# An encoder layer on one core: own PSUM banks for the attention outputs, a second buffer for post-norm scales, longer down steps, and x read directly by ScalarE

## The chip, the cores and the metric

The kernel runs on one core of a Trainium2 chip. The metric is the device time of one execution in microseconds (us), lowest being best. A core has a matrix engine (TensorE, PE in the profile), a vector engine (VectorE, DVE), an engine for functions and copies (ScalarE, ACT), GpSimd (POOL), and SyncE (SP), whose queue issues nearly all transfers from HBM here. Matmul results land in PSUM, which this kernel divides into eight banks of 128 x 512 f32; all else lives in SBUF.

## What is computed

One layer of an encoder for 256 tokens of width 2048. A SwiGLU feed-forward (inner width 5632), a token mixer with 16 heads of 128 (4 of neighbourhood attention, 12 of a mixture of dilated windows), a second feed-forward, and a gated per-layer input, each between two RMS norms with gains:

```python
for i in range(DEPTH):                                  # DEPTH = 1
    f = _swiglu(_rmsnorm(h, ffn1_pre_g[i]), ffn1_w_gate[i], ffn1_w_up[i], ffn1_w_down[i])
    h = h + 0.5 * _rmsnorm(f, ffn1_post_g[i])
    m = _mixer(_rmsnorm(h, mix_pre_g[i]), w_qkv[i], na_rpb[i], out_g[i], w_o[i])
    h = h + _rmsnorm(m, mix_post_g[i])
    f = _swiglu(_rmsnorm(h, ffn2_pre_g[i]), ffn2_w_gate[i], ffn2_w_up[i], ffn2_w_down[i])
    h = h + 0.5 * _rmsnorm(f, ffn2_post_g[i])
    g = jax.nn.sigmoid(_rmsnorm(h, ple_pre_g[i]) @ w_ple_gate[i])
    h = h + _rmsnorm(g * (p[i] @ w_ple_proj[i]), ple_post_g[i])
```

In the mixer, q, k and v come from one projection; the heads' outputs o are normalised per head, scaled by `out_g` and multiplied by `w_o`.

## The kernel before

The tokens stand in two tiles of 128 (t = 0 and 1); the layer's weights, 373 MB with everything, are streamed from HBM once. A **k-tile** is 128 rows of a weight matrix; a product has 512 columns of output at a time, one PSUM bank for each token tile.

*Products.* To keep f32 accuracy, each operand is split into a rounded high part and the low rest. `load_rows` fetches four k-tiles (1 MB) into `raw`; `split` makes `wh` (a cast on ScalarE, L72) and `wl` (a subtraction on VectorE, L73), two k-tiles at a time, six buffers of each. `mac` then does three matmuls per k-tile and token tile (L90 high x high, L91 low x high, L92 high x low). `product` walks over the k-tiles in steps: by default eight k-tiles, a shorter one first if they don't divide. In each step it does t = 0, then t = 1. A caller may give other `steps`, and a job `mid`: that is put into the last step, three k-tiles before t = 1 is done, when t = 0 is complete.

*Pair product.* From the second block on, gate and up of 512 columns each are computed together by `pair_product`, which needs fewer products of half size by adding weights and inputs first, in the manner of Strassen. It has accumulators x, v, z and y, and four times a temporary product named `pair_x` that ScalarE copies out (L174 and a later line) or VectorE adds in. All of them take a bank from the pool `ps_acc`.

*Feed-forward.* `swiglu` goes through 11 blocks of 512 hidden columns in groups of 3, 3, 3 and 2. Behind each group come the down products of its hidden columns, for four blocks b of output columns, with steps of four k-tiles (`KB`) each. `down_out` adds a result to f (L396); in the last group it also sums squares (L232) and multiplies f by the post-norm scale `g_post` (L399), which `gain` loads for each block (L217) into the pool `gpool` with one buffer.

*Seams.* When the last block of t = 0 is complete, `residual` begins: a sum (L225), a power on GpSimd (L226 and L227), h = f*r + h (L328), then `transposed_split`: transposes of h on PE (L239), the product y_g with the next pre-norm gain (L243), and the split into u_h (L245) and u_l (L246), which the next products read. After the first feed-forward the next product is q; after the second it is pp, the product with the per-layer input, which does not read h, and then the gate pg, which does.

*Mixer.* For each of four groups g of four heads, products q, k and v are computed and rotated or scaled, then `attend` runs: for each token tile and pair of heads, scores `sc` (L504), bias and maximum on VectorE (L511), exponentials `pr` on ScalarE (L515), transposes `pt` (L521), a copy `pts` on ScalarE (L523) and the product `o` with v (L527). Scores and transposes share the two banks of `ps_tr`; o takes a bank of `ps_acc`. The result `on` is transposed and split later. Behind the last group stand the products `mo` with `w_o`.

*Start.* The first gate product loads x as it goes (`load_x`, in steps of 1, 1 and seven times 2 k-tiles): xb arrives by DMA, VectorE multiplies it by the gain (xg, L297), ScalarE casts (u_h, L298), VectorE subtracts (u_l, L299). The first two xg are kept for `token_sums`, the input sums of the pair products.

*Order.* The program is written in this sequence, but each engine's order is set by the framework's scheduler from the order of writing, the pools' free buffers and its own priorities. So a pool with another number of buffers can move instructions on an engine.

Of the kernel before, what the change touches and what calls it, by code (L numbers as in the profile page):

```python
# [8 lines left out]
F32 = mybir.dt.float32  # L9
# [6 lines left out]
P = 128  # L16
D = 2048
S = 256
# [15 lines left out]
def encoder_layer(ctx: ExitStack, tc: tile.TileContext, a: dict, out: bass.AP):  # L34
# [9 lines left out]
    resid = ctx.enter_context(tc.tile_pool(name="resid", bufs=1))  # L44
    acts = ctx.enter_context(tc.tile_pool(name="acts", bufs=1))
    wpool = ctx.enter_context(tc.tile_pool(name="wpool", bufs=3))
    gpool = ctx.enter_context(tc.tile_pool(name="gpool", bufs=1))
    work = ctx.enter_context(tc.tile_pool(name="work", bufs=2))
    small = ctx.enter_context(tc.tile_pool(name="small", bufs=4))
    ps_acc = ctx.enter_context(tc.tile_pool(name="ps_acc", bufs=6, space=PSUM))  # L50
    ps_tr = ctx.enter_context(tc.tile_pool(name="ps_tr", bufs=2, space=PSUM))


    ident = const.tile([P, P], F32, name="ident")
# [81 lines left out]
    def pair_product(lhs, sums, wa, ca, wb, cb):  # L136

        a11, a12 = of_tile(lhs[:2], 0), of_tile(lhs[2:4], 0)
        a22 = of_tile(lhs[2:4], 1)  # L150
        s1, s2, s3, s4 = sums
        nk = len(lhs)

        def bank(x):
            return ps_acc.tile([P, NB], F32, name=f"pair_{x}", tag="acc")

        def part(name):
            return ffn_pool[0].tile([P, NB], F32, name=name, tag="part", bufs=6)

        def add(out_, x, y):  # L160
            nc.vector.tensor_tensor(out_, x, y, op=ALU.add)  # L161

        def rest(w, k, c, accs_, first=False, last=False):

            parts = load_parts(w, k * P, 4, c)
            for t, acc in accs_:
                mac(acc, of_tile(lhs[k : k + 4], t), parts, first=first, last=last)

        ra = load_rows(wa, 0, 4, ca, pool=ffn_pool[0], bufs=2)
        rb = load_rows(wb, 0, 4, cb, pool=ffn_pool[0], bufs=2)  # L170
        x = bank("x")
        mac(x, a11, split(ra[:, :2]), first=True, last=True)
        p1 = part("p1")
        nc.scalar.copy(p1, x)  # L174
        add(ra[:, :2], ra[:, :2], rb[:, :2])
        x = bank("x")
        mac(x, s1, split(ra[:, :2]), first=True, last=True)
        r5 = part("r5")
        nc.scalar.copy(r5, x)
        v, z = bank("v"), bank("z")  # L180
        rest(wb, 4, cb, [(1, v), (0, z)], first=True)
        run_later()
        add(ra[:, :2], ra[:, :2], rb[:, 2:])
        x = bank("x")
        mac(x, s2, split(ra[:, :2]), first=True, last=True)
        w_ = part("w")
        add(w_, x, p1)
        mac(z, s4, split(rb[:, 2:]))
        add(rb[:, 2:], rb[:, :2], rb[:, 2:])
        rest(wb, 8, cb, [(1, v), (0, z)])  # L190
        x = bank("x")
# [97 lines left out]
    def load_x(k):  # L289
        if k % 2:  # L290
            return
        hi, lo = (u[:, k % KB : k % KB + 2] for u in x_blocks[k // KB])
        xb = work.tile([P, 2, S], F32, name="xb", tag="hg")
        nc.sync.dma_start(xb, xT[:, k : k + 2])
        xg = work.tile([P, 2, S], F32, name="xg", tag="y0" if k < KB else "sq")
        g = row_g[:, 0, k : k + 2]
        nc.vector.tensor_tensor(xg, xb, g.unsqueeze(2).broadcast_to([P, 2, S]), op=ALU.mult)  # L297
        nc.scalar.copy(hi, xg)  # L298
        nc.vector.tensor_tensor(lo, xg, hi.bitcast(F32), op=ALU.subtract)  # L299
        if k < KB:  # L300
            x_first.append(xg)

    def load_h(k):
        t = k // KB - NT
# [40 lines left out]
    def swiglu(pool, f, ssf, res, blocks, rs, sums, w_gate, w_up, w_down, g_post):  # L345
# [11 lines left out]
        for gi, ng in enumerate(FF_GROUPS):  # L357
            hid = []
            for nb in range(f0, f0 + ng):
# [4 lines left out]
                else:  # L364
                    gate, up = accs("gate"), accs("up")
                    if rs is None:
                        steps = [1, 1] + [2] * 7
                        product(gate, lhs, w_gate, 0, c0, steps=steps, ahead=load_x)
                        a1, a2 = x_first
                        half = [slice(t * P, (t + 1) * P) for t in range(NT)]  # L370
                        sums += token_sums(*(x[:, :, h_] for h_ in half for x in (a1, a2)))
# [15 lines left out]
            for b in range(D // NB):  # L387
# [15 lines left out]
                    if last and b == D // NB - 1:  # L403
                        next(res)

                product(acc, hrows, w_down, f0 * NB, b * NB, steps=[KB] * ng, mid=mid)
                down_out(1)
            f0 += ng

# [15 lines left out]
    with ExitStack() as att:  # L425
# [66 lines left out]
        def attend(qT, kT, v, bias, o_split, g):  # L492

            for t in range(NT):
                tok = slice(t * P, (t + 1) * P)
                o = ps_acc.tile([P, KB, HD], F32, name="o", tag="acc")
                den = small.tile([P, KB], F32, name="den")
                for h0 in range(0, KB, 2):
                    sc = ps_tr.tile([P, 2, S], F32, name="sc", tag="tr")
# [43 lines left out]
                    on, o, ro.unsqueeze(2).broadcast_to([P, KB, HD]), op=ALU.mult  # L543
                )
                on = on.rearrange("p h d -> p (h d)")
                later.append(lambda on=on, t=t: transposed_split(on, *o_split, t, g))

        w_na, w_dil = 4 * HD, 12 * HD
        o_blocks = []
# [182 lines left out]
```

## Time and profile before

| | us |
|---|---|
| three runs | 1986.32, 1985.33, 1981.21 (median 1985.33) |
| the profiled execution | 1985.5 |
| its span from the first to the last instruction | 1983.5 |
| PE busy | 1947.0 (98%) |
| VectorE busy | 1371.2 (69%) |
| ScalarE busy | 992.0 (50%) |
| weights and inputs read from HBM | 373.33 MB, 189 GB/s over the span |

The mean granted clock of TensorE is 0.995. The span divides into the first feed-forward (to about 726 us), the mixer (to about 1146), the second feed-forward (to about 1867) and the per-layer input.

A line of the timeline gives its start and duration in us, the engine, the line of the kernel, the operation, its output and inputs with their shapes, and, in brackets, how long the engine stood idle before it and what released it. A matmul's duration there holds its latency, so that records of neighbours overlap; the pace is the distance of their starts. Names such as `pair_x` or `g_post` are those of tiles in the kernel.

### The profile page before, as it was taken

To read this page: it belongs to the slowest core of one execution; us is meant where nothing else is said; L and a number is where in the kernel's file an instruction comes from. 1 tells how busy PE (TensorE), PEld (TensorE's weight loads), DVE (VectorE), ACT (ScalarE), POOL (GpSimd) and SP (SyncE) were. 2 spreads that over 40 slices of the span, in tenths; PEclk is the share of its full clock that TensorE was granted. 3 is DMA by queue.
4 is the path that set the end of the run, shared out by engine and by line. 5 is a ranking of instruction groups with operands and counts; after the bars stand their busy time and mean duration, and the time that the engine had idled before them with its cause. 6 is when DMAs were issued, how large, how long until landed. Compare 5 with 4: busy or idle time off the path is not lost.

```text
span 1983.5 us, 22804 instructions
## 1 busy us (share of the span) xinstructions
PE 1947.0 (98%) x8840; PEld 1612.7 (81%) x8840; DVE 1371.2 (69%) x1526; ACT 992.0 (50%) x1206; POOL 26.5 (1%) x47
## 2 busy tenths in 40 slices
PE   8999999999999999999999999999999999999998
PEld 6888888888888878788888878888888888888786
DVE  6874787578757776566565587747875787577764
ACT  6554554355435446544535465545543554354563
POOL 0000000000000000000000000000000000000000
PEclk9999999999999999999999999999999999999999
DMA  9666556555655546454453665555565556555453
GB/s 336 212 211 201 170 191 226 177 191 170 233 170 191 191 163 214 130 198 139 138 202 127 219 211 186 210 198 171 191 229 174 191 170 233 170 190 191 170 195 119
DMA packets 190348, 376.91 MB, mean 190 GB/s; under 512 B 6432, under 2 KB 9504, under 8 KB 189984
## 3 DMA queue, kind: packets, MB, share of 16 engines
q1 hardware_dynamic: 190240, 375.46, 55.8%
q8 instruction: 69, 1.13, 0.2%
q14 instruction: 39, 0.32, 0.0%
HBM read 373.33 MB, written 2.10 MB: 189 GB/s over the span
## 4 chain that ended last, share of the span: by engine, by line
PE 95%; DMA 2%; ACT 1%; DVE 1%; issue 0%; POOL 0%; SPq 0%; DVEq 0%; POOLq 0%; ACTq 0%
PE down L90 8%; PE down L91 8%; PE down L92 8%; PE pair_x L90 5%; PE pair_x L91 5%; PE pair_x L92 5%; PE pair_z L92 3%; PE pair_y L90 3%; PE pair_z L90 3%; PE pair_z L91 3%; PE pair_y L92 3%; PE pair_y L91 3%; PE pair_v L90 3%; PE pair_v L91 3%; PE pair_v L92 3%; PE tr L239 2%
## 5 line engine op out<-in xcount | busy, mean ns | idle before, releaser
L73 DVE TENSOR_TENSOR wl<-raw,wh 128x1024 fp32r<-128x1024 f32 (+1 forms) x753 | 908.9, 1221 | 446.0 <-ACT wh L72 421.8
L72 ACT CAST wh<-raw 128x1024 fp32r<-128x1024 f32 (+1 forms) x753 | 790.0, 1052 | 762.2 <-PE down L91 207.9
L90 PE MATMUL down<-wh,hid_h 128*128 128x512 f32 x704 | 274.7, 391 | 0.1
L91 PE MATMUL down<-wh,hid_l 128*128 128x512 f32 x704 | 274.2, 389 | 0.0
L92 PE MATMUL down<-wl,hid_h 128*128 128x512 f32 x704 | 274.2, 389 | 0.0
L90 PEld LDWEIGHTS down<-wh,hid_h 128*128 128x128 f32 x704 | 132.2, 188 | 28.1 <-ACT hid_h L245 1.0
L92 PEld LDWEIGHTS down<-wl,hid_h 128*128 128x128 f32 x704 | 132.2, 188 | 27.4
L91 PEld LDWEIGHTS down<-wh,hid_l 128*128 128x128 f32 x704 | 132.2, 188 | 27.1
L90 PE MATMUL pair_x<-wh,u_h 128*128 128x512 f32 x320 | 124.6, 389 | 0.0
L91 PE MATMUL pair_x<-wh,u_l 128*128 128x512 f32 x320 | 124.6, 389 | 0.0
L92 PE MATMUL pair_x<-wl,u_h 128*128 128x512 f32 x320 | 124.6, 389 | 0.0
L90 PE MATMUL pair_y<-wh,u_h 128*128 128x512 f32 x280 | 109.0, 389 | 0.0
L92 PE MATMUL pair_y<-wl,u_h 128*128 128x512 f32 x280 | 109.0, 389 | 0.0
L91 PE MATMUL pair_y<-wh,u_l 128*128 128x512 f32 x280 | 109.0, 389 | 0.0
L161 DVE TENSOR_TENSOR raw<-raw 128x1024 f32<-128x1024 f32 x80 | 97.8, 1223 | 1.4
L92 PE MATMUL pair_z<-wl,u_h 128*128 128x512 f32 x240 | 93.5, 390 | 0.0
L90 PE MATMUL pair_z<-wh,u_h 128*128 128x512 f32 x240 | 93.4, 389 | 0.0
L91 PE MATMUL pair_z<-wh,u_l 128*128 128x512 f32 x240 | 93.4, 389 | 0.0
L91 PE MATMUL pair_v<-wh,u_l 128*128 128x512 f32 x240 | 93.4, 389 | 0.0
L92 PE MATMUL pair_v<-wl,u_h 128*128 128x512 f32 x240 | 93.4, 389 | 0.0
L90 PE MATMUL pair_v<-wh,u_h 128*128 128x512 f32 x240 | 93.4, 389 | 0.0
L92 PEld LDWEIGHTS pair_x<-wl,u_h 128*128 128x128 f32 x320 | 60.1, 188 | 12.5
(195 smaller groups left out, 3085.3 us busy)
## 6 DMA issues: line engine op xcount, KB each, us to landing
raw<-in_ffn_w_up SPq DMA_DIRECT2D x88, 1024.0 KB, 5.1
raw<-in_ffn_w_down SPq DMA_DIRECT2D x88, 1024.0 KB, 4.9
raw<-in_ffn_w_gate SPq DMA_DIRECT2D x84, 1024.0 KB, 5.1
raw<-in_w_qkv SPq DMA_DIRECT2D x48, 1024.0 KB, 5.1
raw<-in_w_o SPq DMA_DIRECT2D x16, 1024.0 KB, 4.9
raw<-in_w_ple_gate SPq DMA_DIRECT2D x16, 1024.0 KB, 5.0
raw<-in_ffn_w_gate SPq DMA_DIRECT2D x7, 512.0 KB, 4.8
xb<-in_xT SPq DMA_DIRECT2D x8, 256.0 KB, 4.2
```

Of the source, the lines that this page charges most:

```text
L72: nc.scalar.copy(wh[:, :n], raw)
L73: nc.vector.tensor_tensor(wl[:, :n], raw, wh[:, :n].bitcast(F32), op=ALU.subtract)
L90: nc.tensor.matmul(acc, xh, wh, start=lead, stop=False)
L91: nc.tensor.matmul(acc, xl, wh, start=False, stop=False)
L92: nc.tensor.matmul(acc, xh, wl, start=False, stop=tail)
L161: nc.vector.tensor_tensor(out_, x, y, op=ALU.add)
L239: nc.tensor.transpose(tr[:, k], x[:, k * P : (k + 1) * P], ident)
```

## The change

Five things change.

1. `gpool` has two buffers instead of one.
2. `ps_acc` has four banks instead of six, and a new pool `ps_o` has the two others. The attention outputs o take theirs from `ps_o`, and so do the four temporaries of `pair_product` (`pair_x` before, `pair_s` now).
3. `load_x`: the product xg is gone. ScalarE's activation scales xb by the gain and rounds it to u_h, per k-tile, and VectorE gets u_l as xb*g - u_h in one operation per k-tile. The first two xb are multiplied by the gain in place, ahead of `token_sums`.
4. The down products keep steps of four k-tiles only for the first block of columns; the others have the default: 4 and 8 k-tiles in groups of three, 8 in the last group.
5. `on`, transposed, uses another buffer tag (`y0`).

```diff
-    gpool = ctx.enter_context(tc.tile_pool(name="gpool", bufs=1))
+    gpool = ctx.enter_context(tc.tile_pool(name="gpool", bufs=2))
...
-    ps_acc = ctx.enter_context(tc.tile_pool(name="ps_acc", bufs=6, space=PSUM))
+    ps_acc = ctx.enter_context(tc.tile_pool(name="ps_acc", bufs=4, space=PSUM))
     ps_tr = ctx.enter_context(tc.tile_pool(name="ps_tr", bufs=2, space=PSUM))
+    ps_o = ctx.enter_context(tc.tile_pool(name="ps_o", bufs=2, space=PSUM))
...
         def bank(x):
+            if x == "s":
+                return ps_o.tile([P, NB], F32, name="pair_s", tag="o")
             return ps_acc.tile([P, NB], F32, name=f"pair_{x}", tag="acc")
...
-        x = bank("x")
+        x = bank("s")
         mac(x, a11, split(ra[:, :2]), first=True, last=True)
...
-        xb = work.tile([P, 2, S], F32, name="xb", tag="hg")
+        xb = work.tile([P, 2, S], F32, name="xb", tag="y0" if k < KB else "hg")
         nc.sync.dma_start(xb, xT[:, k : k + 2])
-        xg = work.tile([P, 2, S], F32, name="xg", tag="y0" if k < KB else "sq")
-        g = row_g[:, 0, k : k + 2]
-        nc.vector.tensor_tensor(xg, xb, g.unsqueeze(2).broadcast_to([P, 2, S]), op=ALU.mult)
-        nc.scalar.copy(hi, xg)
-        nc.vector.tensor_tensor(lo, xg, hi.bitcast(F32), op=ALU.subtract)
+        for i in range(2):
+            g = row_g[:, 0, k + i : k + i + 1]
+            nc.scalar.activation(hi[:, i], xb[:, i], AF.Copy, scale=g)
+            nc.vector.scalar_tensor_tensor(
+                lo[:, i], xb[:, i], g, hi[:, i].bitcast(F32), op0=ALU.mult, op1=ALU.subtract
+            )
         if k < KB:
-            x_first.append(xg)
+            x_first.append(xb)
...
+                        for i, x in enumerate(x_first):
+                            g = row_g[:, 0, 2 * i : 2 * i + 2].unsqueeze(2).broadcast_to([P, 2, S])
+                            nc.vector.tensor_tensor(x, x, g, op=ALU.mult)
...
-                product(acc, hrows, w_down, f0 * NB, b * NB, steps=[KB] * ng, mid=mid)
+                product(acc, hrows, w_down, f0 * NB, b * NB, steps=[KB] * ng if b == 0 else None, mid=mid)
...
-                o = ps_acc.tile([P, KB, HD], F32, name="o", tag="acc")
+                o = ps_o.tile([P, KB, HD], F32, name="o", tag="o")
...
-                later.append(lambda on=on, t=t: transposed_split(on, *o_split, t, g))
+                later.append(lambda on=on, t=t: transposed_split(on, *o_split, t, g, tag="y0"))
```

The change moves instructions at these places (line numbers after it are larger by 1 to 7: L90 to L92 are L91 to L93, L239 is L242, L504 is L511, L521 is L528, L527 is L534).

PE in the second attention (g = 1), before: the rows from the last scores of the first pair of heads to the second token tile; q stands only further down, behind the third o.

```order
L504 MATMUL sc<-kT_l,qT_h 128x256
L521 MATMUL pt<-ident,pr 128x128 x2
L504 MATMUL sc<-kT_h,qT_h 128x256
L504 MATMUL sc<-kT_h,qT_l 128x256
L504 MATMUL sc<-kT_l,qT_h 128x256
L521 MATMUL pt<-ident,pr 128x128 x2
L504 MATMUL sc<-kT_h,qT_h 128x256
L504 MATMUL sc<-kT_h,qT_l 128x256
L504 MATMUL sc<-kT_l,qT_h 128x256
L527 MATMUL o<-v,pts 128x128 x4
```

The same place now, from the fourth of six q matmuls that stand ahead of the first pt (q is the next group's product, which only reads u and weights):

```order
L91 MATMUL q_6787<-wh,u_h 128x512
L92 MATMUL q_6787<-wh,u_l 128x512
L93 MATMUL q_6787<-wl,u_h 128x512
L528 MATMUL pt<-ident,pr 128x128 x2
L511 MATMUL sc<-kT_h,qT_h 128x256
L511 MATMUL sc<-kT_h,qT_l 128x256
L528 MATMUL pt<-ident,pr 128x128 x2
L511 MATMUL sc<-kT_l,qT_h 128x256
L511 MATMUL sc<-kT_h,qT_h 128x256
L511 MATMUL sc<-kT_h,qT_l 128x256
L511 MATMUL sc<-kT_l,qT_h 128x256
L91 MATMUL q_6787<-wh,u_h 128x512
```

Six q matmuls moved ahead of pt, and further ones stand one by one before and between the groups of o. In the first attention (g = 0) twelve stand ahead of pt.

PE at the end of the second feed-forward, before: the last down matmuls, the products pp with the per-layer input, and the first transposes of the new h.

```order
L91 MATMUL down_13924<-wh,hid_l 128x512
L92 MATMUL down_13924<-wl,hid_h 128x512
L90 MATMUL pp_14038<-wh,p_h 128x512
L91 MATMUL pp_14038<-wh,p_l 128x512
L92 MATMUL pp_14038<-wl,p_h 128x512
L90 MATMUL pp_14038<-wh,p_h 128x512
L91 MATMUL pp_14038<-wh,p_l 128x512
L92 MATMUL pp_14038<-wl,p_h 128x512
L90 MATMUL pp_14039<-wh,p_h 128x512
L91 MATMUL pp_14039<-wh,p_l 128x512
L239 MATMUL tr<-ident,h 128x128 x4
```

The same place now:

```order
L91 MATMUL down_13929<-wh,hid_h 128x512
L92 MATMUL down_13929<-wh,hid_l 128x512
L242 MATMUL tr<-ident,h 128x128 x4
L93 MATMUL down_13929<-wl,hid_h 128x512
L242 MATMUL tr<-ident,h 128x128 x4
L91 MATMUL down_13929<-wh,hid_h 128x512
L92 MATMUL down_13929<-wh,hid_l 128x512
L93 MATMUL down_13929<-wl,hid_h 128x512
L91 MATMUL pp_14043<-wh,p_h 128x512
```

The transposes of the first tile's h moved from behind eight pp matmuls to four matmuls ahead of the end of the down products. The end of the first feed-forward has them at the like place.

VectorE at the start, before:

```order
L297 TENSOR_TENSOR xg<-xb,row_g 128x512 x2
L299 TENSOR_TENSOR u_l<-xg,u_h 128x512
L73 TENSOR_TENSOR wl<-raw,wh 128x512 x2
L299 TENSOR_TENSOR u_l<-xg,u_h 128x512
L73 TENSOR_TENSOR wl<-raw,wh 128x1024
L297 TENSOR_TENSOR xg<-xb,row_g 128x512
L299 TENSOR_TENSOR u_l<-xg,u_h 128x512
L297 TENSOR_TENSOR xg<-xb,row_g 128x512
L73 TENSOR_TENSOR wl<-raw,wh 128x1024
```

And now (y_s and sums_l belong to `token_sums`):

```order
L301 SCALAR_TENSOR_TENSOR u_l<-xb,row_g,u_h 128x256 x2
L375 TENSOR_TENSOR xb<-xb,row_g 128x512
L74 TENSOR_TENSOR wl<-raw,wh 128x512 x2
L301 SCALAR_TENSOR_TENSOR u_l<-xb,row_g,u_h 128x256 x2
L74 TENSOR_TENSOR wl<-raw,wh 128x1024
L301 SCALAR_TENSOR_TENSOR u_l<-xb,row_g,u_h 128x256 x4
L375 TENSOR_TENSOR xb<-xb,row_g 128x512
L258 TENSOR_TENSOR y_s<-xb 128x256
L260 TENSOR_TENSOR y_s<-xb 128x256
L259 TENSOR_TENSOR y_s<-y_s,xb 128x256
L261 TENSOR_TENSOR y_s<-xb,y_s 128x256
L264 TENSOR_TENSOR sums_l<-y_s,sums_h 128x512
```

The token sums moved ahead of the second subtraction of 128x1024 weights; before they stood far behind. On SP the third and fourth load of x are issued earlier, and each `g_post` one place earlier.

More of the change, by code (lines that the diff above doesn't have):

```diff
@@ L175, in pair_product @@
         add(ra[:, :2], ra[:, :2], rb[:, :2])
-        x = bank("x")
+        x = bank("s")
         mac(x, s1, split(ra[:, :2]), first=True, last=True)
@@ L183, in pair_product @@
         add(ra[:, :2], ra[:, :2], rb[:, 2:])
-        x = bank("x")
+        x = bank("s")
         mac(x, s2, split(ra[:, :2]), first=True, last=True)
@@ L190, in pair_product @@
         rest(wb, 8, cb, [(1, v), (0, z)])
-        x = bank("x")
+        x = bank("s")
         mac(x, s3, split(rb[:, 2:]), first=True, last=True)
```

## The prediction

> **What bounds the kernel now.** I read the page's busy times first, then the view of stretches (the windows), then PE's waits grouped by releaser, then the timeline around each wait.
>
> ```profile
> span 1983.5 us, 22804 instructions
> PE 1947.0 (98%) x8840; PEld 1612.7 (81%) x8840; DVE 1371.2 (69%) x1526; ACT 992.0 (50%) x1206; POOL 26.5 (1%) x47
> 0.00:35.00 35.00, 27.15 (x104) 20.98 (x104) 24.20 (x33) 19.12 (x24) 0.73 (x7) 1.00 0.90 307
> 690.00:760.00 70.00, 66.36 (x294) 53.72 (x293) 53.74 (x71) 37.99 (x63) 5.19 (x8) 0.95 0.57 193
> 800.00:825.00 25.00, 21.70 (x121) 18.62 (x120) 11.29 (x30) 13.87 (x28) 2.03 (x2) 0.93 0.27 85
> 1175.00:1850.00 675.00, 674.95 (x3023) 559.69 (x3022) 488.05 (x491) 336.79 (x363) 0.00 (x0) 1.00 0.57 193
> 1850.00:1900.00 50.00, 46.62 (x216) 38.36 (x215) 37.06 (x49) 28.43 (x50) 4.03 (x6) 0.97 0.51 171
> ```
>
> A row of stretches gives its bounds and length, then the busy time of PE, PEld, DVE, ACT and POOL, PE's granted clock, the DMA share and GB/s. TensorE is busy for 98% of the span. Inside the second feed-forward (1175 to 1850) it is busy for 674.95 of 675 us at clock 1.00, so nothing can be had there without fewer matmuls, and the change removes none. What can be won is idle time and half clock at the seams: the start, the end of each feed-forward (690:760 and 1850:1900), and the attentions (800:825 is the first). The clock dips in just these stretches. The prices:
>
> ```profile
> 719.75 0.39 PE L90 MATMUL down<-wh,hid_h 128*128 128x512 f32 x1
> 726.32 0.39 PE L92 MATMUL down<-wl,hid_h 128*128 128x512 f32 x1
> 729.80:733.30 3.50, 2.25 (x6) 1.32 (x7) 3.50 (x7) 1.84 (x4) 0.00 (x0) 0.50 0.01 2
> 733.80 0.63 PE L90 MATMUL q<-wh,u_h 128*128 128x512 f32 x1
> 734.23 0.63 PE L91 MATMUL q<-wh,u_l 128*128 128x512 f32 x1
> ```
>
> The first two are the first and last of 30 matmuls in a row: 6.57 us over 29 steps, **0.2266 us per matmul**. At clock 0.50 the step is 0.43, so each matmul loses 0.20.
>
> **The change part by part.** Let T be the end of the last down matmul, 726.55 in the first feed-forward.
>
> *End of the first feed-forward.* PE's next work there is q, whose input needs the finished h.
>
> ```profile
> 724.03 0.69 DVE L396 TENSOR_TENSOR f<-f,down 128x512 f32<-128x512 f32 x1 [0.63 <-PE down L92]
> 726.17 0.15 DVE L225 TENSOR_REDUCE m<-ssf 128x1 f32<-128x4 f32 x1
> 728.17 1.41 DVE L328 SCALAR_TENSOR_TENSOR h<-f,r,h 128x512 f32<-128x512 f32 x2 [0.44 <-POOL r L227]
> 729.02 1.71 PE L239 MATMUL tr<-ident,h 128*128 128x128 f32 x8 [2.31 <-issue]
> 730.10 1.37 DVE L243 TENSOR_TENSOR y_g<-tr,row_g 128x512 f32<-128x512 f32 x2
> 731.56 0.80 PE L90 MATMUL q<-wh,u_h 128*128 128x512 f32 x1 [0.82 <-ACT u_h L245]
> 732.78 0.80 PE L91 MATMUL q<-wh,u_l 128*128 128x512 f32 x1 [0.42 <-DVE u_l L246]
> 737.43 0.60 PE L239 MATMUL tr<-ident,h 128*128 128x128 f32 x4
> ```
>
> The first token tile's sums end before the last 12 matmuls now (4 k-tiles of 3), and before the last 24 with a last step of 8 k-tiles. The whole chain of that tile therefore starts 12 x 0.2266 = 2.72 us earlier: reduce at T-3.1, h at T-1.1, first transpose at T-0.25 instead of T+2.5. The order puts three h updates ahead of y_g instead of two, so y_g stands at T-1.1+3x0.69 = T+1.0 (was T+3.55), q's first matmul 1.46 behind that at T+2.4 (was T+5.0). Before u_l DVE now does two y_g, the second tile's f and one h (2.1 and 0.7): u_l at T+3.7, the second q matmul at T+4.4 (was T+6.2). Up to the second tile's transposes 15 q matmuls stand (13 now): PE is there at T+4.4+14x0.23 = T+7.6 if warm, 1.4 later if seven of these are at half clock; now it is at 737.43 = T+10.9. That is 3.3 or 1.9 less, and two matmuls more (0.45): 3.7 or 2.3. A transpose that waits for one of the two banks that scores and transposes share may cost 0.7. Its price isn't in the trace, so bounds: **2.6 us, between 1.6 and 3.7**. The idle time left is about 2 us ahead of q and 1.6 behind its first matmul, near to the 2.31 and 0.82 that brought clock 0.50, so I lean to the half clock. The Trainium skill, "TensorE: Matmul & The Clock Gate", section "Part 1: The HAM clock gate", says that the gate falls to half only after an idle window of about 3.4 us; by that no half clock would come here, and this term would be its upper end. The trace differs: PE was idle 2.5 us and then 1.2 when it fell at 729.8.
>
> *The four attentions.* Now o takes two of six accumulator banks, and q of the next group has none free until o is read. With banks of its own for o, q's matmuls can fill the holes.
>
> ```profile
> 805.09 0.28 PE L504 MATMUL sc<-kT_l,qT_h 128*128 128x256 f32 x1
> 808.07 0.47 PE L521 MATMUL pt<-ident,pr 128*128 128x128 f32 x2 [2.70 <-ACT pr L515]
> 808.10:811.80 3.70, 3.67 (x17) 3.37 (x18) 0.78 (x4) 1.93 (x7) 0.00 (x0) 0.54 0.99 323
> 887.26 0.28 PE L504 MATMUL sc<-kT_l,qT_h 128*128 128x256 f32 x1
> 888.82 0.44 PE L521 MATMUL pt<-ident,pr 128*128 128x128 f32 x2 [1.28 <-ACT pr L515]
> 890.51 1.16 PE L527 MATMUL o<-v,pts 128*128 128x128 f32 x8 [0.32 <-ACT pts L523]
> 895.84 1.16 PE L527 MATMUL o<-v,pts 128*128 128x128 f32 x8 [0.38 <-ACT pts L523]
> 887.00:897.00 10.00, 7.83 (x60) 6.94 (x59) 5.74 (x22) 7.52 (x21) 0.36 (x1) 1.00 0.67 210
> ```
>
> In the first attention the order puts 12 q matmuls before the first pt, and five more one by one before the third o. The first fill the hole of 2.70 (12 x 0.2266 = 2.72), the five fill the holes ahead of o: 17 x 0.2266 = 3.85 us. The 3.7 us at clock 0.54 behind the hole go too; I take a third of them as lost, since the rest would be spent waiting for ScalarE's copies anyway: 1.2. In the second attention, on which the two others are modelled, six stand before pt (1.36 for the hole of 1.28), and five later, where the o rows show 0.32 and 0.38 of idle time. 11 x 0.2266 = 2.5; the stretch 887 to 897 leaves 10.00-7.83 = 2.2 idle, and a busy row also counts the tail of a matmul that nothing follows, so 2.5 fits in. Together 3.85+1.2+3x2.5 = **12.6 us, between 7.7** (only the holes ahead of pt: 2.70+1.2+3x1.28) **and 13.3** (half of the dip, 1.9, in place of a third). Behind the fillers the first pt comes no later than pr is ready: 1.36 against 1.28+0.1. The weights that they need are cast while v's matmuls run, and k's banks are read by copies before the attention starts.
>
> *End of the second feed-forward.* PE's next work is pp, which needs no h.
>
> ```profile
> 1859.31 0.34 SPq L217 DMA_DIRECT2D g_post<-in_ffn_post_g  x1
> 1868.49 0.69 DVE L399 TENSOR_TENSOR f<-f,g_post 128x512 f32<-128x512 f32 x1 [3.68 <-DMA g_post<-in_ffn_post_g]
> 1871.99 0.63 PE L239 MATMUL tr<-ident,h 128*128 128x128 f32 x4 [3.38 <-DVE h L328]
> 1873.84 0.63 PE L92 MATMUL pp<-wl,p_h 128*128 128x512 f32 x1
> ```
>
> With one buffer, the last scale's DMA goes out at 1859.3, once the scale before is used, and f waits 3.68 for it. With two it goes out a block earlier, 48 matmuls or 10.9 us: with the 9.1 from its issue to f's start it is there at about 1857.6, five before its use. Now PE loses the 3.38 of its wait and 0.2 on each of 9 matmuls at half clock (1.8): 5.2. With the scale on time h comes as in the other feed-forward at T-1.1 and the transposes at T-0.2, where PE is at T-0.9 by the order: about 0.8 idle. Then four wl subtractions and a transpose bank may hold y_g up for 0.5 to 0.9, while pp's matmuls run. Gain 5.2-0.8-0.7 = **3.7, between 2** (half clock after all, 1.8 again) **and 5** (no wait).
>
> *Start.*
>
> ```profile
> 6.11 0.80 PE L90 MATMUL gate<-wh,u_h 128*128 128x512 f32 x1 [6.11 <-ACT wh L72]
> 8.12 0.80 PE L91 MATMUL gate<-wh,u_l 128*128 128x512 f32 x1 [1.22 <-DVE u_l L299]
> L297 DVE TENSOR_TENSOR xg<-xb,row_g 128x512 f32<-128x512 f32 x8 | 5.5, 691 | 7.4 <-DMA xb<-in_xT 7.3
> L298 ACT CAST u_h<-xg 128x512 fp32r<-128x512 f32 x8 | 5.0, 622 | 8.1 <-DVE xg L297 8.1
> L255 DVE TENSOR_TENSOR y_s<-xg 128x256 f32<-128x256 f32 x1 | 0.4, 422 | 0.0
> 807.41 0.51 ACT L515 ACTIVATE pr<-sb,nmax 128x256 f32<-128x256 f32 x1
> ```
>
> The product with g leaves DVE (8 x 0.69), ScalarE does two activations of 128x256 (0.51 each, by L515) where it did one cast of 0.62 (+0.4 x 8), DVE two operations of 0.42 for one of 0.69, and two multiplies in place (1.4). The 1.22 wait for u_l can go. But the first matmul stays at 6.11, held by the weights, and the DMA share of 0.90 in the first 35 us says that the weights set the pace there; and the order now puts the in-place multiplies and the token sums ahead of the fourth step's subtraction, some 3.7 us of DVE (2 x 0.69 and 4 x 0.42 and the 0.69 of a subtraction), though what x costs there per step falls too. On SP's queue two loads of x are issued ahead of weights that stood before them, which moves weights by 0.5 MB at most. **0.3 us, between -1.4** (the multiplies in place fully on the path) **and +1.2** (the wait for u_l fully won).
>
> *At nothing:* the mixer's end (its last step was 8 long already, and stays), the other buffer tag of the transposed o, and the pair products' four temporaries in the o banks. The last ones pay only if their ScalarE copy comes late (below).
>
> Sum: 2.6+12.6+3.7+0.3 = 19.2. The profiled execution took 1985.5 (span 1983.5 and 2.0 around it), 0.2 over the median: 1985.5-19.2 = **1966**. The low ends sum to 9.9 (1976), the high ends to 23.2 (1962).
>
> **Rivals.**
> *The fillers pay nothing:* q, begun early, only waits later for its weights, since pr and pts stand on ScalarE between its casts, and the attention term is lost: 1985.5-6.6 = 1979. For it: ACT is busy for 7.52 of 10 us in the second attention. Against it: PE never waits for wh there now, and the fillers use up two of six pairs that stand cast.
> *The seams gain nothing:* DVE has the third h and the second tile's f ahead of what q needs, or the new transposes hold PE up while down matmuls stand behind them; 12.6+0.3 = 12.9 remain: 1972.6. For it: the order does both. Against it: 2.7 us of lead.
> *No half clock behind the first feed-forward:* the holes there shrink from 2.5 and 1.2 us to about 2 and 1.6, under what halved the clock. The term is 3.7 in place of 2.6: 1965. This is what the Trainium skill's rule above would make of it.
> *Slower:* the third temporary of each pair product waits for the copy of the first, with two banks in place of a share of six.
>
> ```profile
> 56.92 0.59 ACT L174 COPY p<-pair_x 128x512 f32<-128x512 f32 x1 [0.93 <-PE pair_x L92]
> 64.31 0.48 PE L90 MATMUL pair_x<-wh,sums_h 128*128 128x512 f32 x1
> ```
>
> The copy ends at 57.5, the third temporary begins at 64.3: 6.8 us of slack. If the six weight casts queued ahead of it (1.36 us apart at full pace, 8.2) ran first, each of 20 pair products would wait 1.4 us: +28, less 19, **1994**. It decides from a copy 6.8 us late. The order on ScalarE leaves the copy where it was, so I give it little. The Trainium skill, same page, section "A second HAM failure mode: psum-queue depth-cycling", warns that cycling through PSUM banks makes PE idle briefly and the clock swing; by that these short waits would cost half clock too. No run here shows it: the clock is 1.00 over 675 us.
>
> **How the numbers follow.** Forecast 0.52 (1962 to 1976), no half clock 0.2 (1965, inside), seams gain nothing 0.1 (1972.6, inside), fillers pay nothing 0.12 (1979), slower 0.04, less than 0.02 for anything else. I reach from 1959, three under the lowest sum, since the runs shown range over 5, to the highest, 1976: left out are the 1979 and the slower case, 0.16, and a few hundredths of spread. A measurement of this kernel tells 0.3% (6 us) from no change: the 1979 case stands on that edge (1979.4) and is halved. Faster 0.52+0.2+0.1+0.06 = 0.88 and most of the rest, 0.9; same 0.06; slower 0.04.
>
> **What would show it.** Right: no wait of PE for pr over 0.3 us, clock 1.00 at 800:825, f's wait for g_post gone, the first transposes of h within 1 us of T, pair products without a wait of PE between their temporaries. Wrong: q idle for wh behind the attentions, half clock there, or a PE wait with ACT p L177 as releaser.

## The result and the profile after

| | median us (runs) | ratio to before, 95% interval |
|---|---|---|
| before | 1984.55 (4) | |
| after | 1967.57 (4, 1967.0 to 1969.0) | 0.9917 (0.99 to 0.9935) |

The change is 17.0 us faster; 1966 was predicted. The profiled execution of after took 1969.0 us, the slowest of its four. From its page, the first two lines, and its view of stretches (columns as before):

```profile
span 1967.0 us, 22810 instructions
PE 1943.0 (99%) x8840; PEld 1607.8 (82%) x8840; DVE 1369.4 (70%) x1528; ACT 993.6 (51%) x1214; POOL 28.3 (1%) x47
0.00:35.00 35.00, 26.97 (x104) 21.17 (x105) 22.50 (x35) 19.23 (x31) 0.73 (x7) 1.00 0.88 302
690.00:760.00 70.00, 67.47 (x302) 54.42 (x301) 54.08 (x71) 37.72 (x65) 6.56 (x8) 0.98 0.58 195
800.00:825.00 25.00, 25.00 (x146) 21.12 (x145) 14.03 (x33) 17.79 (x32) 2.03 (x2) 1.00 0.27 86
1850.00:1900.00 50.00, 48.97 (x232) 40.32 (x231) 39.32 (x52) 34.44 (x60) 4.29 (x8) 1.00 0.60 210
```

The same number of matmuls, less idle time. The first attention (800 to 825) has no hole (idle stretch of PE) left and its clock is 1.00 (21.70 us busy and 0.93 before). The end of the second feed-forward is at 1.00 too; only the end of the first still has a dip (0.98). The start shows no gain: 26.97 us busy of 35 against 27.15.

Lines of the timeline of after, from the end of the first feed-forward (PE, VectorE, ScalarE), the first attention (PE) and the end of the second feed-forward (VectorE, PE):

```profile
727.86 0.63 PE L242 MATMUL tr<-ident,h 128*128 128x128 f32 x4 [0.50 <-issue]
729.00 1.28 DVE L246 TENSOR_TENSOR y_g<-tr,row_g 128x512 f32<-128x512 f32 x2
729.76 1.04 ACT L73 CAST wh<-raw 128x1024 fp32r<-128x1024 f32 x1 [1.95 <-PE down L92]
730.71 1.13 ACT L248 CAST u_h<-y_g 128x512 fp32r<-128x512 f32 x2
731.38 0.50 PE L91 MATMUL q<-wh,u_h 128*128 128x512 f32 x1 [1.47 <-ACT u_h L248]
732.20 0.50 PE L92 MATMUL q<-wh,u_l 128*128 128x512 f32 x1 [0.32 <-DVE u_l L249]
...
807.32 0.39 PE L93 MATMUL q<-wl,u_h 128*128 128x512 f32 x1
807.67 0.44 PE L528 MATMUL pt<-ident,pr 128*128 128x128 f32 x2
...
1850.23 0.69 DVE L406 TENSOR_TENSOR f<-f,g_post 128x512 f32<-128x512 f32 x1 [0.85 <-ACT sq L235]
1853.74 0.63 PE L242 MATMUL tr<-ident,h 128*128 128x128 f32 x4 [0.55 <-DVE h L332]
```

At the end of the first feed-forward PE's waits for h, u_h and u_l went from 2.31, 0.82 and 0.42 to 0.50, 1.47 and 0.32; ahead of u_h stands a cast of weights on ScalarE. In the attention, pt follows q without a wait; the 2.70 us are full of q matmuls. At the end of the second feed-forward f waits for ScalarE's squares (0.85) and no longer for the scale (3.68), and PE waits 0.55 for h in place of 3.38.

**Where the 16.5 us between the two profiles come from.** I take the start of a matmul that has the same work ahead of it in both kernels, subtract 0.2266, 0.1133 or 0.0567 us for each matmul of 512, 256 or 128 columns ahead of it, and so get the time that PE has lost by then. The difference to the profile of before, by stage (negative is gained; "start" is to the first pair product, FF1 and FF2 are the two feed-forwards):

| kernel | start | end of FF1 | attentions 1, 2, 3, 4 | end of FF2 and rest | sum |
|---|---|---|---|---|---|
| predicted | -0.3 | -2.6 | -5.05, -2.5, -2.5, -2.5 | -3.7 | -19.2 |
| after | +1.6 | -2.0 | -4.9, -2.4, -2.7, -2.4 | -3.7 | -16.5 |
| after, second profile (e12_again) | -0.1 | -2.2 | -4.9, -2.4, -2.7, -2.4 | -3.7 | -18.5 |
| e1_ps | +0.6 | +1.9 | -4.9, -2.4, -2.4, -2.4 | -0.2 | -10.0 |
| e2_steps | +0.4 | -1.9 | -1.1, 0.0, 0.0, 0.0 | -2.6 | -5.3 |
| e3_gain | -0.1 | +1.1 | +0.1, 0.0, 0.0, 0.0 | -3.9 | -2.8 |
| e4_steps_gain | -0.8 | -1.9 | -1.2, 0.0, 0.0, +1.6 | -3.7 | -6.0 |

Rows without the edit that matters for a stage show how much a stage varies by itself: the end of the first feed-forward up to 1.9 in a kernel that leaves it alone (e1_ps), the first attention by 1.2, the fourth by 1.6. In each of these cases the half clock came at another place, or once more or less often (see "The clock" below).

### The profile page after: what moved, and what is told of

It is laid out like the page before. It is cut to its first block, busy times and chain, and to the rows that moved or that the text cites. A ratio compares the mean times of both kernels' runs of the same rounds, so it can differ in the third digit from the quotient of the medians.

```text
span 1967.0 us, 22810 instructions
## 1 busy us (share of the span) xinstructions
PE 1943.0 (99%) x8840; PEld 1607.8 (82%) x8840; DVE 1369.4 (70%) x1528; ACT 993.6 (51%) x1214; POOL 28.3 (1%) x47
## 4 chain that ended last, share of the span: by engine, by line
PE 95%; DVE 2%; DMA 1%; ACT 1%; issue 1%; POOL 0%; SPq 0%; DVEq 0%; POOLq 0%; ACTq 0%
PE down L91 8%; PE down L93 8%; PE down L92 8%; PE pair_z L93 3%; PE pair_y L93 3%; PE pair_x L93 3%; PE pair_z L91 3%; PE pair_x L91 3%; PE pair_y L91 3%; PE pair_z L92 3%; PE pair_x L92 3%; PE pair_y L92 3%; PE pair_v L93 3%; PE pair_v L91 3%; PE pair_v L92 3%; PE pair_s L92 2%
## 5 line engine op out<-in xcount | busy, mean ns | idle before, releaser
L91 PE MATMUL down<-wh,hid_h 128*128 128x512 f32 x704 | 274.7, 391 | 0.1
L93 PE MATMUL down<-wl,hid_h 128*128 128x512 f32 x704 | 274.1, 389 | 0.0
L92 PE MATMUL down<-wh,hid_l 128*128 128x512 f32 x704 | 273.9, 389 | 0.0
L91 PEld LDWEIGHTS down<-wh,hid_h 128*128 128x128 f32 x704 | 132.1, 188 | 28.1 <-ACT hid_h L248 1.0
L93 PEld LDWEIGHTS down<-wl,hid_h 128*128 128x128 f32 x704 | 132.1, 188 | 27.3
L92 PEld LDWEIGHTS down<-wh,hid_l 128*128 128x128 f32 x704 | 132.2, 188 | 27.1
L91 PE MATMUL pair_y<-wh,u_h 128*128 128x512 f32 x280 | 108.9, 389 | 0.0
L92 PE MATMUL pair_y<-wh,u_l 128*128 128x512 f32 x280 | 108.9, 389 | 0.0
L93 PE MATMUL pair_y<-wl,u_h 128*128 128x512 f32 x280 | 108.9, 389 | 0.0
L91 PE MATMUL pair_x<-wh,u_h 128*128 128x512 f32 x280 | 108.9, 389 | 0.0
L92 PE MATMUL pair_x<-wh,u_l 128*128 128x512 f32 x280 | 108.9, 389 | 0.0
L93 PE MATMUL pair_x<-wl,u_h 128*128 128x512 f32 x280 | 108.9, 389 | 0.0
L93 PE MATMUL pair_z<-wl,u_h 128*128 128x512 f32 x240 | 93.4, 389 | 0.0
L91 PE MATMUL pair_v<-wh,u_h 128*128 128x512 f32 x240 | 93.4, 389 | 0.0
L92 PE MATMUL pair_v<-wh,u_l 128*128 128x512 f32 x240 | 93.4, 389 | 0.0
L93 PE MATMUL pair_v<-wl,u_h 128*128 128x512 f32 x240 | 93.4, 389 | 0.0
L91 PE MATMUL pair_z<-wh,u_h 128*128 128x512 f32 x240 | 93.4, 389 | 0.0
L92 PE MATMUL pair_z<-wh,u_l 128*128 128x512 f32 x240 | 93.4, 389 | 0.0
L403 DVE TENSOR_TENSOR f<-f,down 128x512 f32<-128x512 f32 x48 | 32.8, 683 | 44.6 <-PE down L93 44.6
```

The source lines that it names most:

```text
L91: nc.tensor.matmul(acc, xh, wh, start=lead, stop=False)
L92: nc.tensor.matmul(acc, xl, wh, start=False, stop=False)
L93: nc.tensor.matmul(acc, xh, wl, start=False, stop=tail)
L403: nc.vector.tensor_tensor(f_t, f_t, acc[t], op=ALU.add)
```

## The experiments

### Each part alone: e1_ps, e2_steps, e3_gain, e4_steps_gain

All four change the kernel before.

```diff
 e1_ps
-    ps_acc = ctx.enter_context(tc.tile_pool(name="ps_acc", bufs=6, space=PSUM))
+    ps_acc = ctx.enter_context(tc.tile_pool(name="ps_acc", bufs=4, space=PSUM))
+    ps_o = ctx.enter_context(tc.tile_pool(name="ps_o", bufs=2, space=PSUM))
...
-                o = ps_acc.tile([P, KB, HD], F32, name="o", tag="acc")
+                o = ps_o.tile([P, KB, HD], F32, name="o", tag="o")
 e2_steps, e4_steps_gain
-                product(acc, hrows, w_down, f0 * NB, b * NB, steps=[KB] * ng, mid=mid)
+                product(acc, hrows, w_down, f0 * NB, b * NB, steps=[KB] * ng if b == 0 else None, mid=mid)
 e3_gain, e4_steps_gain
-    gpool = ctx.enter_context(tc.tile_pool(name="gpool", bufs=1))
+    gpool = ctx.enter_context(tc.tile_pool(name="gpool", bufs=2))
```

> Only the PSUM division is changed against the kernel before (o and the pair products' temporaries in two banks of their own). Theory: it carries the whole attention term by itself, because q of the next group only lacked a bank. From the start of q's product ahead of an attention to the next k product PE then loses about 12.4 us less over the four attentions (4.9, 2.4, 2.7, 2.4 as between the two kernels), and nothing else changes: first matmul at 6.1, f's wait of 3.7 for g_post at the end of the second feed-forward still there; time 1984.5-12.4 = 1972. Rival 1: the scheduler needs the other edits too (the tag of the transposed o), and q moves less: 1976 to 1984. Rival 2: the pair products wait for their two banks, and that is hidden in the full change by gains elsewhere: PE waits on ScalarE's copies of the temporaries, time above 1975.

Measured: 1974.60 us, ratio 0.9941 (0.9926 to 0.9955), against 1986.04 on the same chip: 11.4 us. The four attentions gain 12.1 in the trace (table), as in the full change, and the stretch of the first one is full:

```profile
800.00:825.00 25.00, 25.00 (x143) 21.05 (x142) 11.21 (x30) 16.30 (x31) 2.03 (x2) 1.00 0.34 115
```

So the PSUM division carries the attention term by itself. The other tag for the transposed o isn't needed for it.

> Only the longer down steps are changed against the kernel before. Theory: the earlier end of the first token tile is held back by the one g_post buffer: at the end of the first feed-forward f*g_post is wanted at T-3.7, but the last scale landed only 2.1 us ahead of T, so at most 1 us is gained there; at the end of the second the scale lands 1.8 behind T and nothing is gained. Time 1983.5 to 1984.5, and VectorE's waits for g_post grow at both places. Rival (the steps work alone): 2.0 at the first end and 0.9 or more at the second: 1981.5.

Measured: 1980.20, ratio 0.9971 (0.9961 to 0.9981): 5.8 us, where I expected one at most. My theory fell. Of the 5.3 in the trace 1.9 and 2.6 stand at the two ends, where the rival had 2.0 and "0.9 or more"; 1.1 is the half clock of the first attention, which did not come. VectorE's timeline at the end of the second feed-forward, in before and then in e2_steps:

```profile
1868.49 0.69 DVE L399 TENSOR_TENSOR f<-f,g_post 128x512 f32<-128x512 f32 x1 [3.68 <-DMA g_post<-in_ffn_post_g]
1869.10 0.15 DVE L225 TENSOR_REDUCE m<-ssf 128x1 f32<-128x4 f32 x1
```

```profile
1860.33 0.16 DVE L225 TENSOR_REDUCE m<-ssf 128x1 f32<-128x4 f32 x1 [0.85 <-ACT sq L232]
1861.44 1.42 DVE L328 SCALAR_TENSOR_TENSOR h<-f,r,h 128x512 f32<-128x512 f32 x2 [0.95 <-POOL r L227]
1863.71 0.69 DVE L399 TENSOR_TENSOR f<-f,g_post 128x512 f32<-128x512 f32 x1 [0.85 <-DMA g_post<-in_ffn_post_g]
```

The scale still comes late (0.85 of wait), but f*g_post of the last block now stands behind the sum and two h updates, not ahead of them. Neither needs it: the sum is over squares taken before the scale, and these h are of other blocks. In the profile before, the sum began only behind f*g_post: VectorE stood idle for 3.68 us until the scale came, and with it a chain that had no use for the scale.

At the first end a single trace says little, since that stage varies by 1.9. But all kernels with the longer steps gained there against before (0.6 to 2.5 in eight traces; e6_warm and e10_shift128, whose down products are slower, are left out), and the three others without them lost (0.6 to 1.9).

> Only the second buffer for the post-norm scales is changed against the kernel before. Theory: nothing at the end of the first feed-forward (there f*g_post waited for ScalarE's squares); at the end of the second f*g_post comes 2.7 to 2.8 us earlier (now T+1.85), PE's wait of 3.38 for h shrinks to about 0.6, and the half clock behind it (1.8) goes: 4.6 gained, 1980. Rival: the half clock stays, or PE waits elsewhere instead: 2.8 gained, 1981.7. If this alone gains as much as the full change does at that place (3.7), the longer steps add nothing there.

Measured: 1982.75, ratio 0.9984 (0.9975 to 0.9993): 3.3 us. In e3_gain f*g_post waits for squares alone, and PE's wait for h is 0.50 instead of 3.38:

```profile
1866.81 0.69 DVE L399 TENSOR_TENSOR f<-f,g_post 128x512 f32<-128x512 f32 x1 [0.85 <-ACT sq L232]
...
1870.27 0.63 PE L239 MATMUL tr<-ident,h 128*128 128x128 f32 x4 [0.50 <-DVE h L328]
```

The half clock behind it is gone too, as in the theory. By the table the second buffer alone wins 3.9 at that place, less than the 4.6 of the theory and as much as the full change (3.7).

> Longer down steps and the second scale buffer together, against the kernel before. Theory: each needs the other at the first end: 2.0 gained there (half clock included) and 3.7 at the second, 1984.5-5.7 = 1979, first transposes of h four matmuls ahead of T at both ends. Rival (they add up without help): the sum of the two single runs, and no more at the first end than the steps alone.

Measured: 1979.51, ratio 0.997 (0.9957 to 0.9983): 6.5 us. At the second end it wins 3.7, like the buffer alone; at the first 1.9, like the steps alone. So the theory had the sizes right, but not the reason: at the first end the steps need no second buffer. The rival was right there, and wrong at the second end, where 2.6 and 3.9 don't add up. The two ends give 5.6 in this trace, where the prediction had 6.3; that 6.5 was timed is a chance agreement, since the start and two attentions differ from before as well (-0.8, -1.2 and +1.6).

### The start: e5_loadx, e8_no_loadx

```diff
 e5_loadx (the kernel before with the new load of x), e8_no_loadx (the changed kernel with the old one)
-        nc.vector.tensor_tensor(xg, xb, g.unsqueeze(2).broadcast_to([P, 2, S]), op=ALU.mult)
-        nc.scalar.copy(hi, xg)
+            nc.scalar.activation(hi[:, i], xb[:, i], AF.Copy, scale=g)
```

> Only the loading of x is changed against the kernel before. Theory: it costs, since ScalarE's table load of 1.28 us, which stood at 0.7 us ahead of everything, now stands behind x's transfer (4.3) and ahead of the first u_h: first matmul at 7.1 instead of 6.1, and another 0.5 lost in the up product; PE is 1.5 us behind at the first pair product, time 1986. Rival (the prediction): the wait for u_l won and a gain of 0.3: 1984.3.

> The changed kernel with the loading of x as before. Theory: the start as before (first matmul 6.1) and everything else as in the changed kernel: 1.5 less, 1966.0, or 1964.4 if the shift also takes the half clock at the end of the first feed-forward away. Rival (the load edit gains by its second half, the shorter work on VectorE): 1967.6 or more.

Measured: e5_loadx 1985.62, ratio 0.9995 (0.9986 to 1.0004) to before; e8_no_loadx 1967.66, ratio 0.9909 (0.9894 to 0.9924), where the changed kernel has 0.9917 (0.99 to 0.9935). A gain of 0.3 can't be told from nothing. The loss of 1.5 that I expected lies outside e5_loadx's interval (0.8 at most), and e8_no_loadx can't tell. The traces say why so little comes of it. ScalarE's start before, and then after:

```profile
0.71 1.28 ACT L298 ACT_TABLE_LOAD   x1 [0.71 <-PEq L722]
```

```profile
4.34 1.28 ACT L300 ACT_TABLE_LOAD   x1 [4.34 <-DMA xb<-in_xT]
5.64 0.91 ACT L300 ACTIVATE u_h<-xb,row_g 128x256 fp32r<-128x256 f32 x2
7.11 0.79 PE L91 MATMUL gate<-wh,u_h 128*128 128x512 f32 x1 [7.11 <-ACT wh L73]
```

The new first activation depends on two transfers, x and the gains. One of the waits stands on the table load ahead of it, so that 1.28 us of loading, which before were done by 2.0, begin when x has come. The first matmul starts at 6.6 to 7.1 in the traces with this load (after, e5, e7, e10, e11, e12) and at 5.9 to 6.2 in those with the old one (before, e1 to e4, e8). The means are 0.8 apart. But the first pair product starts at 54.4 to 56.9, mean 55.6, against 54.6 to 55.9, mean 55.4: on the mean 0.6 of the 0.8 comes back on the way, though with so wide a spread that is no more than likely. After's own +1.6 was the worst of six draws.

### The table load set free: e6_warm, e9_warm_m, and what an address costs: e10_shift128, e11_shift256

```diff
 e6_warm
+    warm = small.tile([P, 1], F32, name="warm")
+    nc.scalar.copy(warm, row_g[:, 0, :1])
 e9_warm_m
+    warm = small.tile([P, 1], F32, name="m")
+    nc.scalar.copy(warm, row_g[:, 0, :1])
 e10_shift128 ([P, 16] in e11_shift256)
+    pad = small.tile([P, 1], F32, name="pad")
+    nc.gpsimd.memset(pad, 0.0)
     xT = a["xT"].rearrange("(k p) s -> p k s", p=P)
```

> The changed kernel, plus a copy of one column of row_g on ScalarE ahead of everything: it takes the wait for the gains, so that the table load stands free at 0.7 us. Theory: first matmul back at 6.1 and 1.0 gained up to the first pair product (0.5 of the 1.5 stays, in the up product): 1966.5. Of the half clock at the end of the first feed-forward, which fell in a window of 3.41 us from 733.1 whose predecessor held 1.65 and 0.6 us of idle PE: if the clock looks at windows on a fixed grid from the program's start, the 1 us shift spreads this idle time over two windows, the half clock goes and another 1.6 with it: 1965. If it looks at the length of the waits alone, the half clock stays. Rival: the table load was hidden by the weights' transfer anyway, first matmul still at 7.1 and nothing gained: 1967.6.

Measured: 1978.89, ratio 0.9964 (0.9949 to 0.9978): 11 us slower than after. The start did as expected (first matmul 5.5, first pair product 54.0), but from there the kernel fell behind by the same amount with every down and mo product and never in a pair product. The new tile of four buffers had moved all buffers behind it in SBUF by 128 bytes a partition. Three kernels were made to tell it apart.

> As e6_warm (the changed kernel with an early copy on ScalarE that takes the wait for the gains), but the copy goes into a tile that is there already, so that no buffer in SBUF moves. Theory: the 11 us that e6_warm lost came from the new tile's 128 bytes alone, which moved every buffer behind it; the pace of the down matmuls is back at 0.2266 and the table load is free: first pair product at 54 instead of 55.2 to 56.9, time 1966 to 1967. Rival 1: the slow pace came from the extra ScalarE instruction or the order: 1978 again. Rival 2: the table load is worth nothing behind the weights' transfer: 1967.6.

> The changed kernel with an unused tile of 128 bytes a partition, set to zero once by GpSimd at the start: nothing else than addresses moves (hid_h from 175616 to 175744, which is 128 off a multiple of 256). Theory: down and mo matmuls run at 0.2322 instead of 0.2266 us (0.0056 x 2112 down and some 380 mo matmuls, 12 to 14 us): 1979 to 1981. Rival (the address has no part in it): 1967.6.

> The same with an unused tile of 256 bytes (hid_h at 175872, a multiple of 256 but not of 512). Theory: if what counts is a multiple of 256 bytes, the pace is 0.2266 and the time 1967.6; if it is one of 512, 0.2322 and 1979 to 1981 again.

Measured: e9_warm_m 1965.11, ratio 0.9899 (0.9884 to 0.9914); e10_shift128 1980.96, 0.9977 (0.9966 to 0.9987); e11_shift256 1967.59, 0.9912 (0.9892 to 0.9931). The costliest groups of e10_shift128, then of e11_shift256:

```profile
L91 PE MATMUL down<-wh,hid_h 128*128 128x512 f32 x704 | 278.6, 396 | 0.1
...
L91 PE MATMUL pair_y<-wh,u_h 128*128 128x512 f32 x280 | 109.0, 389 | 0.0
```

```profile
L91 PE MATMUL down<-wh,hid_h 128*128 128x512 f32 x704 | 274.6, 391 | 0.1
```

The records of down matmuls grew from 391 to 396 ns, their distance from 0.2267 to 0.2325 us; pair products, whose inputs lie ahead of the new tile, kept 389. hid, the stationary operand of these matmuls, starts by the built program at 175616 bytes in after, 175744 with the pad of 128 and 175872 with that of 256. So a start that is 128 off a multiple of 256 made these matmuls 2.6% slower, and one that is 256 off a multiple of 512 cost nothing. The extra copy isn't the cause: e9_warm_m has it and keeps the old pace, e10_shift128 is slow without it. Of the operands of a down matmul only hid moved, since the weights' buffers lie ahead of the new tile; that it is hid's place that counts is inferred from this, and why it should matter is open.

e9_warm_m, whose copy uses a tile that is there anyway, **beats both kernels**: 3.1 us less than the changed kernel on the same chip (1968.22, e12_again below), with no run in common. Its start:

```profile
0.71 1.28 ACT L288 ACT_TABLE_LOAD   x1 [0.71 <-PEq L731]
2.45 0.19 ACT L288 COPY m<-row_g 128x1 f32<-128x1 f32 x1 [0.45 <-DMA row_g<-in_row_gT]
3.94 0.91 ACT L302 ACTIVATE u_h<-xb,row_g 128x256 fp32r<-128x256 f32 x2 [1.30 <-DMA xb<-in_xT]
5.84 0.80 PE L91 MATMUL gate<-wh,u_h 128*128 128x512 f32 x1 [5.84 <-ACT wh L73]
```

The first pair product starts at 53.8 (54.0 in e6_warm), 1.7 ahead of the mean of the others with this load; so much the table's place costs. Against the mean with the old load it is 1.5: so much the new load is worth with the table out of the way. PE's wait for the first u_l is 0.7 there (1.2 in before), and the 0.5 that it waited for wl in the up product is gone.

### The temporaries' banks: e7_pair_acc

```diff
-        x = bank("s")
+        x = bank("x")
```

in the four places, so that the temporaries share the four accumulator banks again.

> The changed kernel, but the pair products' four temporaries take their banks from the four accumulator banks again; the attention outputs keep their own two. Theory: four banks are too few for x, v, z, y and what the last pair product still holds, so PE waits for ScalarE's and VectorE's readings in each of the 20 pair products, 0.5 to 2 us each: 1977 to 2007. This is the price at which the division would have been slower. Rival: the readings come in time, nothing changes: 1967.6; then the temporaries' own banks carry nothing.

Measured: 1968.36, ratio 0.9913 (0.9898 to 0.9928); nothing changes, and the second feed-forward stays full in e7_pair_acc:

```profile
1175.00:1850.00 675.00, 674.95 (x3023) 559.54 (x3022) 486.32 (x492) 334.21 (x363) 0.00 (x0) 1.00 0.57 191
```

Four banks are enough here even for the whole pair product. The theory of this run fell, and the prediction's slower rival has no ground here.

### The clock, and the changed kernel again: e12_again

> The changed kernel itself, for a second profile. Theory: the half clock comes by a grid of windows of 3.413 us whose place against the program differs from execution to execution, after a window in which PE stood idle for 2.4 us or more. The hole at the end of the first feed-forward is about that long, so the half clock of the first profile there is a matter of the grid: it comes only where one window holds 2.4 us of it, and without it the span is 1.6 shorter. Rival: it belongs to the kernel and comes each time.

Measured: 1968.22, ratio 0.9916 (0.9899 to 0.9932); in its profile, span 1965.0, there is no half clock at the end of the first feed-forward. The places where the clock changes lie on a grid of 3.413 us within one execution, and the grid lies differently against the program in each (2.79, 2.63 and 2.43 us behind its start in before, after and e12_again, modulo 3.413; 0.19 in e2_steps). Windows of that grid, of before, of after and of e12_again:

```profile
726.41:729.83 3.42, 1.03 (x7) 0.55 (x6) 2.88 (x4) 1.11 (x2) 1.64 (x2) 1.00 0.43 167
729.83:733.24 3.41, 2.16 (x6) 1.25 (x7) 3.41 (x6) 1.84 (x4) 0.00 (x0) 0.50 0.01 2
```

```profile
729.66:733.08 3.42, 1.62 (x7) 0.92 (x6) 3.42 (x7) 2.71 (x5) 0.00 (x0) 1.00 0.00 0
733.08:736.49 3.41, 3.41 (x10) 2.64 (x9) 2.69 (x5) 0.00 (x0) 1.64 (x2) 0.50 0.40 97
```

```profile
726.05:729.46 3.41, 2.04 (x12) 1.46 (x12) 3.41 (x6) 1.46 (x3) 0.00 (x0) 1.00 0.00 0
729.46:732.88 3.42, 2.94 (x12) 2.23 (x13) 3.33 (x6) 1.25 (x4) 1.10 (x1) 1.00 0.01 5
```

In after one window holds nearly the whole hole (1.62 busy of 3.42) and the next has half clock; in e12_again the hole falls on two windows (2.04 and 2.94 busy) and the clock stays. So the rival, by which it comes each time, fell. For a rule I count, in each window of the grid, the time that is left when each matmul is given its pace from its start (0.2266 us and so on, as in the table above). Over the fourteen traces, without their first 20 us and what follows the last matmul, full clock goes to half after all nine windows with 2.5 us or more of such time, after two of five with 2.3 to 2.5, and never with less. What ends a dip after one window or after two, I can't tell.

That the dip's absence would shorten the span by 1.6 was wrong, though the span is 2.0 shorter: 1.7 of that is the start, and the end of the first feed-forward is only 0.3 better. PE's later waits there in e12_again:

```profile
734.36 0.63 PE L242 MATMUL tr<-ident,h 128*128 128x128 f32 x4 [0.47 <-issue]
749.39 0.50 PE L93 MATMUL q<-wl,u_h 128*128 128x512 f32 x1 [0.85 <-DVE wl L74]
```

At full clock PE comes to the second tile's transposes sooner, but then waits 0.47 ahead of them and 0.85 for weights that VectorE has yet to split; in after the first of these waits is missing and the second is 0.2. So between these two profiles the half clock mostly filled time that PE would have waited anyway.

## Why the prediction was right, step by step

**What bounds the kernel:** right. The seams gave everything; the stretch from 1175 to 1850 is as full as it was. One reading was wrong: the clock is not below 1.00 in all of the seams' rows, that of the start (0:35) has 1.00.

**The attentions:** 12.6 forecast, 12.4 in after's trace, 12.1 with the division alone. The size of each attention was right to 0.2. The 1.2 put on the first dip is a matter of the grid: in e2_steps and e4_steps_gain, with o's banks as before, the dip fell out and 1.1 was won.

**The end of the second feed-forward:** 3.7 forecast and measured, with 0.55 of wait for h where 0.8 was told. But I gave the result to the scale and the longer steps together; the second buffer alone gives it, and the steps alone 2.6, with the changed place of f*g_post on VectorE.

**The end of the first:** 2.6 forecast, 2.0 measured with a half clock and 2.2 without (e12_again). The bounds had 2.3 with one and 3.7 without, so the price of the half clock, 1.4, is the part that was wrong: the waits behind it were left out. With T = 728.1 (726.98 and five matmuls, without the transposes between), the first transposes stand at T-0.25 and y_g at T+0.9, as told; q's first matmul at T+3.3 in place of T+2.4, since ScalarE casts weights ahead of u_h; the second at T+4.1 (4.4 forecast), and the second tile's transposes at 737.12 = T+9.0, just what the half clock was to make of them. In e12_again (T = 726.35) they come at T+8.0, after 0.47 of wait, where T+7.6 was told. The half clock, left open between row and the Trainium skill's rule ("TensorE: Matmul & The Clock Gate", section "Part 1: The HAM clock gate"), came in after's profile and not in the next. The free-running window of that page of the Trainium skill is what the traces show; its "idle window" need not be one without work: a window with 1.62 us of busy PE was enough here.

**The start:** the step that failed. That "the first matmul stays at 6.11, held by the weights" left out that ScalarE's table load would move behind x's transfer. The gain of 0.3 that was forecast came near what the traces show on the mean, a loss of 0.2 (by trace between a gain of 1.0 and a loss of 1.6 against before), only by luck: two errors cancel, the table's place (1.7) and too little credit for VectorE's relief (1.5 with the table out of the way, in e9_warm_m and e6_warm).

**The rivals:** fillers that pay nothing, seams without gain and temporaries that wait are refuted by e1_ps, e4_steps_gain and e7_pair_acc. "No half clock behind the first feed-forward" came true in e12_again, but did not bring its 3.7. **The signs** came as told: no wait of PE for pr, clock 1.00 at 800:825, no wait of f for g_post, the first transposes at T-0.25 and T-0.2, no wait between the temporaries. **The sum** of 19.2 came out as 17.0 to 17.8 in timed runs (11.4 and 6.5 for the PSUM division and the two seam edits timed by themselves). The profiles' 16.5 and 18.5 differ by their starts (1.7); what lacks to 19.2 there is in the start and the first end, not in the attentions.

## What to carry to other kernels

When PE idles behind ScalarE while independent matmuls are due, look whether they only lack a PSUM bank: two own banks for the short-lived output were worth 11 us of 17 here, and the temporaries that shared the six banks did not miss them. When a late load holds up a chain, ask whether the chain needs it at all or merely stands behind it in the order of its engine. And before a kernel is called slower by an edit, compare the pace of its matmuls: 128 bytes of a new tile cost more than most edits here gain.

## What the hardware showed beside that

- With the stationary operand's place in SBUF 128 bytes off a multiple of 256, 128x512 f32 matmuls went from 0.2267 to 0.2325 us a piece (e10_shift128, and e6_warm alike; 13 us in all).
- The half clock followed a window of 3.413 us with 2.5 us or more without matmuls, on a grid that differs from execution to execution. The profile before has three such dips; its runs ranged over 8 us on all chips (1981.2 to 1989.0), those of the changed kernel, with one dip in one of two profiles, over 2 (1967.0 to 1969.0, eight runs). The mean granted clock of the runs goes with their time: four runs of the kernel before had 0.993 and took 1987.6 to 1989.0, two had 0.997 and took 1982.7 to 1982.9, and one window at half clock takes 0.0009 off the mean. That the dips make the range was not tried by itself.
- An activation that waits for two transfers let its table load wait for one of them: 1.28 us moved from 0.71 to 4.34.
